# Operand loads of two output projections and row loads of a convolution's tail issued one step ahead, and one tail begun later, in a one-layer fp32 decoder kernel

## The chip, the cores and the metric

The kernel runs on 1 core of one Trainium2 chip. The metric is the device time of one execution in microseconds (us). Three runs of the kernel before gave 2037.54, 2042.94 and 2036.72 us; their median is 2037.54.

The engines have short names in the profile: PE is the matmul engine (PEld its weight loads), DVE the vector engine, ACT the scalar engine, POOL the GpSimd engine, SP the engine whose instruction stream issues most DMAs. A name with a q, such as SPq or ACTq, is the queue from which an engine issues DMAs. Each engine runs its own instructions in the order in which they stand; engines wait for each other on semaphores.

## The reference

One decoder layer over 2048 rows of 1024 values, all float32. Shortened:

```python
hn    = rms_norm(x, mix_pre_g)
proj  = hn @ w_in                               # q, k, v and the convolution's GLU input
attn  = sliding_window_attention(q, k, v, ...)  # window 128, 8 heads, 512 columns
conv  = silu(layer_norm(depthwise_conv31(a * sigmoid(gate)))) @ w_conv_pw   # 512 columns
mixed = concatenate([attn, conv]) @ w_out
h     = x + rms_norm(mixed, mix_post_g)
hn    = rms_norm(h, ffn_pre_g)
ff    = (silu(hn @ w_gate) * (hn @ w_up)) @ w_down
out   = h + rms_norm(ff, ffn_post_g)
```

## The kernel before

The 2048 rows are four tiles of T = 512 rows, numbered 0 to 3. A matmul of float32 accuracy is made of three: each operand is split into a rounded high part (ACT, `AF.Copy`) and a remainder (DVE or POOL, a subtraction), and high x high, high x low and low x high are added up in one PSUM bank.

The names of the stages are labels that the program gives to its tiles. A0 to A3 are the input projections. T0 to T3 are the convolution's taps: 30 multiply-adds per chunk of 128 channels on DVE, four chunks per tile; a finished chunk is stored to a DRAM array `y_scr` (L570). C0 to C3 are the convolution's tails. B is the attention. W0 to W3 are the output projections with their norms, N1 and N3 the later part of such a norm. F0 is the first half of the feed-forward for tiles 0 and 1, G0 the second half (`stage_p2`, L1103), F2 and G2 the same for tiles 2 and 3. H2 prepares operands of F2.

The change lies in what runs beside G0. G0 makes 7 products of 11 steps each, so 77 steps; in a step it loads one block from `mids` (L1122, tiles fa@G and at@G) and, every other step, two from `td` or `w_down` (L1126, mb@G), splits them (two ACT copies, two DVE subtractions, hl@G) two steps ahead, and multiplies with 12 matmuls, three into each of four banks. After the last step of a product, `after` (in `stage_p2`) empties the four banks by copies or additions on DVE and ACT (p@G, x@G) before the next product may write there. The product that ends with step 65 is emptied by additions into x@G on DVE.

Work of other stages runs between the steps in *lanes*. A lane holds a list of generators. Each step of the main stage gives every lane some time (`pump`, about L1275): the lane has a credit that grows by this time multiplied by its rate, and it resumes its first generator while the credit is positive. What a generator yields is taken off the credit. So `yield 0.5` is a price that decides how much main work passes before the next piece. A lane's item may have a condition: `since(lane, name, d)` holds when that item of that lane ended at least d of this planned time ago. These prices set the order in which instructions are emitted; a scheduler of the tile framework orders each engine's instructions with a model of its own. It decides the order in the queues on the chip.

While G0 runs, the lane `lw` holds in this order C2, W2, C3, W3, B11.2 (part of H2), and N3 is added by W3. The lane `lc` runs the last taps, T3.

**The tail, `stage_tail` (L573) and `conv_tail` (L588).** For each of four chunks it loads a row block from `y_scr` into a tile fc@C (L582, 256 KB on SP's queue), transposes it with four matmuls (`turn`, L550 to L557, PE line L554, ct@C) and copies the bank to yt@C (L555). Then `conv_tail` takes mean and variance on DVE (L594, L595), a reciprocal square root (`rsqrt`, L150, on POOL when `beside_taps`, lines L159 to L162), waits for its lane, transposes back (L607), applies the activation and multiplies by `w_pw` (four products `three`), whose results go to the DRAM array `mixT` through ACT's queue.

**The output projection, `stage_w` (L693).** It goes through the 8 chunks of mixT (four of the attention, four of the convolution) in groups of G = 2. For a group, `acts` loads two blocks at@W from `mixT` (L702, SP's queue, 256 KB each), copies the high part (L704, ACT, ql@W) and subtracts the low part (DVE). Each group has two column halves n = 0, 1 of `block_half` (L667): for each of four row groups, six matmuls into a bank tr@W, which is copied or added into mid@W (L675 and DVE). The weights raw@W and w@W are loaded by `weight` (L140).

**The norm, `norm_w` (L732).** It loads the gain gb@W (L684), sums squares (L738, ACT), takes `rsqrt` (on POOL for tiles 0 to 2, on DVE for tile 3), scales with eight DVE operations (`post_scale`, L688: mid@W<-mid@W,sm@W,gb@W), adds rows of x (L757, L759), stores h (h_scr), sums squares again (L760), and takes a second `rsqrt`. `stage_h_plain` (L814) reads such rows back transposed (tr@H, L800), and stores hT<-gb@H (L821) from tiles gb, of which there are two, shared with gb@W.

**The outputs of G0, `finish` (L1081):** norms the pairs of rows, loads h back (wx@G, L1095) and stores `out` (L1099).

The constants: CS = 10 is the planned time between the end of a tile's taps and the start of its tail (the condition on C3), Q0 = 8 the number of early units of F0 that run within W1.

Of the kernel before, what the change touches and what calls it, by code (L numbers as in the profile page):

```python
# [26 lines left out]
T = 512  # L27
NT = S // T
KC = D // P
# [8 lines left out]
def layer_kernel(ctx, tc, x, xT, cols, rows, sinks, relb, onehot, w_in, w_pw, w_out, w_gate, w_up, w_down, out):  # L38
    nc = tc.nc
# [7 lines left out]
    lab = ["X0"]  # L47
# [7 lines left out]
    def t_(tag, shape, dt=F32):  # L55
        return sb.tile(list(shape), dt, tag=tag, name=nm(tag), bufs=BUFS[tag])

    def f4(tag, shape=(P, D)):
        return t_(tag, shape)

    def f2(tag, shape=(P, T)):
        return t_(tag, shape)

    def hl(tag):
        return t_(tag, (P, 2, T), F32R)
# [74 lines left out]
    def weight(src, low, made, raw=None, on_pool=True):  # L140
        if raw is None:
            raw = t_("raw", (P, 2, T))
            nc.sync.dma_start(raw, src)
        return [split_w(raw[:, n], "w", low[n], made, on_pool) for n in range(2)]
# [85 lines left out]
    mixT = dr.tile([KC, P, S], F32, name="mixT")  # L230
# [17 lines left out]
    y_scr = dr.tile([4, P, S], F32, name="y_scr")  # L248
# [301 lines left out]
    def turner(yt, ycs):  # L550
        def turn(c):
            b = ct()
            for s in range(4):
                nc.tensor.transpose(b[:, s * P : (s + 1) * P], ycs[c][:, s * P : (s + 1) * P], ident)  # L554
            act(yt[:, :, c * P : (c + 1) * P], b.rearrange("p (s c) -> p s c", c=P), AF.Copy)  # L555

        return turn  # L557
# [15 lines left out]
    def stage_tail(t):  # L573
        L = f"C{t}"
        lab[0] = L
        yt = t_("yt", (P, 4, 4 * P))
        ycs = []
        turn = turner(yt, ycs)
        for c in range(4):
            lab[0] = L  # L580
            y = f2("fc")
            nc.sync.dma_start(y, y_scr[c, :, t * T : (t + 1) * T])  # L582
            ycs.append(y)
            turn(c)
            yield 0.5
        yield from conv_tail(t, yt)

    def conv_tail(t, yt):  # L588
        L = f"C{t}"
        lab[0] = L  # L590
        mv = sm(8).rearrange("p (s a) -> p s a", a=2)
        for s in range(4):
            st = sm(6)
            nc.vector.bn_stats(st, yt[:, s])  # L594
            nc.vector.bn_aggr(mv[:, s], st)  # L595
        r = rsqrt(mv[:, :, 1], 4, 1.0)
        nmr = sm(4)
        stt(nmr, mv[:, :, 0], -1.0, r, ALU.mult, ALU.mult)
        yield YL if t < 2 else YL2
        lab[0] = L  # L600
        for s in range(4):
            act(yt[:, s], yt[:, s], AF.Identity, scale=r[:, s : s + 1], bias=nmr[:, s : s + 1])
        sc = []
        for c in range(4):
            b = ct()
            for s in range(4):
                nc.tensor.transpose(b[:, s * P : (s + 1) * P], yt[:, s, c * P : (c + 1) * P], ident)  # L607
            th = f2("fc")
            act(th, b, AF.Tanh, scale=lnh[:, c : c + 1], bias=lnh[:, 4 + c : 5 + c])
            v = f2("fc")  # L610
            act(v, b, AF.Identity, scale=ln_g[:, c : c + 1], bias=ln_b[:, c : c + 1])
            stt(v, th, 1.0, v, ALU.add, ALU.mult)
            h = hl("chl")
            act(h[:, 0], v, AF.Copy)
            ptt(h[:, 1], v, h[:, 0].bitcast(F32), ALU.subtract)
            sc.append(h)
            yield 2
            lab[0] = L
        for m in range(4):
            raw = f2("fc")  # L620
            nc.sync.dma_start(raw, w_pw[m])
            w = split_w(raw, "mb" if t == 1 and m % 2 else "chl").rearrange("p a (k c) -> p a k c", c=P)
            o = ct()
            three(o, [((w[:, 0, k], w[:, 1, k]), (sc[k][:, 0], sc[k][:, 1])) for k in range(4)])
            z = f2("gb" if t > 1 else "fc")
            act(z, o, AF.Copy, scale=0.5)
            nc.scalar.dma_start(mixT[4 + m, :, t * T : (t + 1) * T], z)
            yield 2
            lab[0] = L
# [37 lines left out]
    def block_half(acc, units, n, first, L, bank_of, s0=0):  # L667
        cs = slice(n * T, (n + 1) * T)
        for i in range(len(acc)):
            s = i + s0  # L670
            lab[0] = L
            o = bank_of()
            three(o, [((a[s // 4][:, 0, ss(s)], a[s // 4][:, 1, ss(s)]), (w[:, 0], w[:, 1])) for a, w in units])
            if first:
                act(acc[i][:, cs], o, AF.Copy)  # L675
            else:
                vtt(acc[i][:, cs], acc[i][:, cs], o, ALU.add)
            yield 0.65 * len(units)
# [14 lines left out]
    def stage_w(w, spill, G, atag, htag, mtag, bank_of, norm=None, ready=None):  # L693
        L = f"W{w}"
        lab[0] = L
        acc = [f4(atag) for _ in range(4)]

        def acts(gi):
            aa = []
            for c in range(G * gi, G * gi + G):  # L700
                m = f2(mtag)
                nc.sync.dma_start(m, mixT[c, :, w * T : (w + 1) * T])  # L702
                a = hl(htag)
                act(a[:, 0], m, AF.Copy)  # L704
                vtt(a[:, 1], m, a[:, 0].bitcast(F32), ALU.subtract)
                aa.append([a])
            return aa

        nxt = acts(0)
        for gi in range(KC // G):  # L710
            aa = nxt
            for n in range(2):
                lab[0] = L
                if n == 1 and gi + 1 < KC // G and not (ready and G * gi + G == 4):
                    nxt = acts(gi + 1)
                ws = weight(w_out[2 * gi : 2 * gi + 2, :, n * T : (n + 1) * T].rearrange("c p t -> p c t"),
                            lo_out[n, 2 * gi : 2 * gi + 2], w > 0)
                yield from block_half(acc, list(zip(aa, ws)), n, gi == 0, L, bank_of)
            if ready and G * gi + G == 4:
                for i, c in enumerate(ready()):  # L720
                    if i == Q0 // 2:
                        ld.until("C1")
                        lab[0] = L
                        nxt = acts(gi + 1)
                    yield c
        tail = norm_w(w, spill, acc, mtag)
        if norm:
            norm(tail)
        else:
            yield from tail  # L730
# [526 lines left out]
    def since(lane, name, dt):  # L1257
        return name in lane.done and clk[0] >= lane.done[name] + dt
# [51 lines left out]
    TAPS0 = 6  # L1310
    NWARM = 9
    FILL = (2, 2, 2, 2, 2, 1, 0, 0)
    CS = 10
    YC = 3
    YP = 1.5
    YL, YL2 = 12, 20
# [5 lines left out]
    Q0 = 8  # L1322
# [5 lines left out]
    lc = Lane(RC0, LC)  # L1328
    lw = Lane(RW0, 0)
# [19 lines left out]

    lb.add("X", stage_x(), lambda: "x1" in started)  # L1350
    lw.add("W0", stage_w(0, True, 2, "x", "hl", "fa", mm), lambda: "A3" in started and "C0" in ld.done)
    TGA = [["hl"] * 8, ["mid"] * 4 + ["chl"] * 4, ["hl"] * 8, ["mid"] * 4 + ["hl"] * 4]
    xa = {}
# [6 lines left out]
    for t in range(2):  # L1360
        ld.add(f"C{t}", stage_tail(t), lambda t=t: since(lc, f"T{t}", CS))
    for t in range(NT):
# [39 lines left out]
    for n, off in (("B11", 0), ("B21", 4)):  # L1402
        lh.add(n + ".0", stage_h_plain(ws, ops, n, off))
    run(stage_w(1, True, 2, "mid", "hl", "at", mm, norm=lambda g: lh.add("N1", g), ready=lambda: stage_pre(ws, ops, mids[0], keeps[0], 0, Q0)))
    lc.hold = lambda: "S0" not in lh.done
    lh.until("B21.0")
# [6 lines left out]
    lc.rates["T3"] = RC3  # L1413
    ws, ops = (2, 3), {}
    lw.add("C2", stage_tail(2))
    lw.add("W2", stage_w(2, True, 2, "mid", "ql", "at", tr))
    lw.add("C3", stage_tail(3), lambda: since(lc, "T3", CS))
    lw.add("W3", stage_w(3, True, 2, "mid", "ql", "at", tr, norm=lambda g: lw.add("N3", g)))
    lw.add("B11.2", stage_h_plain(ws, ops, "B11", 0))
    run(stage_p2((0, 1), mids[0], td))  # L1420
# [70 lines left out]
```

## Time and profile before

| | us |
|---|---|
| median of 3 runs | 2037.54 |
| runs, lowest to highest | 2036.72 to 2042.94 |
| the profiled execution | 2046.33 |
| its span, first to last instruction | 2044.6 |
| granted TensorE clock, mean over the span | 0.984 |

Durations and times of the trace are those of the one profiled execution; a time such as 1202.57 counts in us from the start of the span. In a timeline row the columns are start, duration, engine, source line, operation, output<-inputs, shapes, and the number of instructions drawn together; in square brackets stand the idle time of the engine before them and what ended it. L85 and L108 are lines of helpers: every DVE operation through `dve` and every matmul of a three-part product have these lines, so the tile names tell them apart. The letter behind the @ is the stage without its number.

The profile has the kernel read 330.60 MB from HBM and write 119.02 MB, 220 GB/s over the span.

### The profile page before, as it was taken

How to read it: one execution, taken by the hardware profiler on the slowest of the kernel's cores; microseconds unless marked ns; L12 is line 12 of the kernel's file. 1: busy time of each engine (PE TensorE's matmuls, PEld its weight loads, DVE VectorE, ACT ScalarE, POOL GpSimd, SP SyncE). 2: the span in 40 equal slices, each digit the busy share in tenths (PEclk: the TensorE clock that was granted, in tenths of full speed). 3: DMA queues.
4: the chain of work that ended last, by engine and by line, in shares of the span. 5: the costliest groups of instructions: out<-in, count | busy, mean ns of one | idle time of the engine just before them, and what ended most of it. 6: DMA issues, size and time to landing. Idle time of an engine off the chain costs nothing. (4 is left out here: it accounts for less than half of the span.)

```text
span 2044.6 us, 27163 instructions
## 1 busy us (share of the span) xinstructions
PE 1961.9 (96%) x8826; PEld 1569.7 (77%) x8826; DVE 1501.3 (73%) x2641; ACT 986.3 (48%) x1938; POOL 399.3 (20%) x442
## 2 busy tenths in 40 slices
PE   8999999999989999999989999989999999999997
PEld 6877766776667778787878778877788888888886
DVE  5999896995885799888649985576756665545558
ACT  5355455456546633333346457555733433345543
POOL 4011223333111300000001012104523333221001
PEclk9999999999999999999999999999999999999999
DMA  8787645678559877777386788579954453366654
GB/s 307 255 300 232 203 135 184 184 240 277 186 156 326 272 239 241 257 247 244 130 263 209 229 266 279 191 278 302 348 169 161 149 169 114 103 235 214 206 186 149
DMA packets 235902, 451.44 MB, mean 221 GB/s; under 512 B 23496, under 2 KB 49264, under 8 KB 235760
## 3 DMA queue, kind: packets, MB, share of 16 engines
q1 hardware_dynamic: 215216, 419.30, 62.6%
q10 hardware_dynamic: 20544, 30.42, 4.0%
q8 instruction: 69, 1.13, 0.2%
q14 instruction: 73, 0.60, 0.1%
HBM read 330.60 MB, written 119.02 MB: 220 GB/s over the span
## 5 line engine op out<-in xcount | busy, mean ns | idle before, releaser
L85 DVE SCALAR_TENSOR_TENSOR fc@C<-glu@C,colt,fc@C 128x512 f32<-128x512 f32 x480 | 368.7, 781 | 3.5
L108 PE MATMUL mm@F<-hl@H,w@F 128*128 128x512 f32 x1056 | 255.2, 393 | 3.6 <-ACT mm@F L909 3.6
L108 PE MATMUL mm@G<-hl@G,hl@G 128*128 128x512 f32 x924 | 229.0, 397 | 9.8 <-DVE x@G L85 5.4
L108 PEld LDWEIGHTS mm@F<-hl@H,w@F 128*128 128x128 f32 x1056 | 200.4, 190 | 45.9 <-ACT mm@F L909 4.1
L108 PE MATMUL mm@A<-hl@A,w@A 128*128 128x512 f32 x840 | 206.9, 398 | 6.0 <-ACT w@A L133 1.7
L108 PEld LDWEIGHTS mm@G<-hl@G,hl@G 128*128 128x128 f32 x924 | 173.9, 191 | 48.6 <-ACT hl@G L782 7.9
L782 ACT ACTIVATE w@F<-chl@F 128x512 fp32r<-128x512 f32 x220 | 135.6, 625 | 148.9 <-PE mm@F L108 140.7
L108 PE MATMUL mm@G<-w@G,hl@G 128*128 128x512 f32 x876 | 199.6, 389 | 0.8 <-DVE w@G L85 0.8
L108 PEld LDWEIGHTS mm@G<-w@G,hl@G 128*128 128x128 f32 x876 | 164.4, 188 | 35.2 <-DVE w@G L85 1.2
L108 PEld LDWEIGHTS mm@A<-hl@A,w@A 128*128 128x128 f32 x840 | 155.9, 189 | 42.6 <-DVE hl@A L85 2.4
L85 DVE TENSOR_TENSOR w@F<-chl@F,w@F 128x512 fp32r<-128x512 f32 x198 | 144.9, 734 | 34.7 <-ACT w@F L782 34.3
L108 PE MATMUL mm@F<-mid@H,w@F 128*128 128x512 f32 x528 | 133.2, 396 | 3.3 <-ACT mm@F L909 3.3
L108 PE MATMUL mm@F<-ql@H,w@F 128*128 128x512 f32 x528 | 127.8, 390 | 5.8 <-ACT w@F L782 5.7
L108 PE MATMUL mm@F<-p@H,w@F 128*128 128x512 f32 x528 | 132.3, 397 | 0.0
L108 PE MATMUL mm@F<-x@H,w@F 128*128 128x512 f32 x528 | 127.4, 395 | 2.3 <-ACT fa@F L931 2.3
L108 PEld LDWEIGHTS mm@F<-ql@H,w@F 128*128 128x128 f32 x528 | 98.8, 188 | 27.3 <-ACT w@F L782 6.5
L108 PEld LDWEIGHTS mm@F<-mid@H,w@F 128*128 128x128 f32 x528 | 99.2, 189 | 26.4 <-ACT mm@F L909 5.4
L108 PEld LDWEIGHTS mm@F<-x@H,w@F 128*128 128x128 f32 x528 | 99.8, 190 | 24.0 <-ACT fa@F L931 2.8
L108 PEld LDWEIGHTS mm@F<-p@H,w@F 128*128 128x128 f32 x528 | 101.2, 192 | 22.1 <-ACT at@F L1031 0.8
L108 PE MATMUL mm@W<-w@W,hl@W 128*128 128x512 f32 x384 | 102.4, 412 | 7.6 <-ACT hl@W L704 7.3
L133 ACT ACTIVATE w@A<-raw@A 128x512 fp32r<-128x512 f32 x110 | 67.6, 626 | 84.4 <-PE mm@A L108 52.4
L108 PE MATMUL tr@W<-w@W,ql@W 128*128 128x512 f32 x384 | 98.5, 395 | 5.8 <-ACT mid@W L675 4.6
(299 smaller groups left out, 3376.9 us busy)
## 6 DMA issues: line engine op xcount, KB each, us to landing
mids<-fa@F SPq DMA_DIRECT2D x154, 256.0 KB, 2.7
raw@A<-w_in SPq DMA_DIRECT2D x55, 512.0 KB, 4.6
w@A<-lo_in SPq DMA_DIRECT2D x84, 256.0 KB, 3.5
fc@G<-mids SPq DMA_DIRECT2D x77, 256.0 KB, 3.4
fa@G<-mids SPq DMA_DIRECT2D x75, 256.0 KB, 4.5
gb@F<-keeps SPq DMA_DIRECT2D x72, 256.0 KB, 4.6
raw@W<-w_out SPq DMA_DIRECT2D x32, 512.0 KB, 5.6
w@W<-lo_out SPq DMA_DIRECT2D x48, 256.0 KB, 4.1
```

Of the source, the lines that this page charges most:

```text
L85: r = op(*args, **kw)
L108: r = nc.tensor.matmul(*args, **kw)
L133: act(w[:, 0], raw, AF.Copy)
L782: act(w[:, 0], x, AF.Copy)
```

## The change

Three edits.

1. `stage_tail`, for tiles 2 and 3 (`t > 1`): the load of the first chunk is issued alone, then the generator yields 2.0. In each turn the load of the next chunk is issued before the transposes of the present one. A turn yields 1.0 instead of 0.5.
2. `stage_w`: `acts` is cut into `loads` (the DMAs) and `acts` (the splits). For tiles 2 and 3 (`w > 1`) the generator yields 4.0 between the first loads and the first splits, and for each later group the loads are issued with the first column half (n = 0) of the group before, the splits with its second half (n = 1). For tiles 0 and 1 both stay at n = 1. In tile 1's special path (`ready`) the loads stay at unit Q0 // 2 = 4 and the splits move to unit Q0 - 2 = 6.
3. C3 may start 16 instead of 10 of planned time after T3 (`CS3`).

```diff
@@ stage_tail
+        def fetch(c):
+            if c < 4:
+                lab[0] = L
+                ycs.append(f2("fc"))
+                nc.sync.dma_start(ycs[c], y_scr[c, :, t * T : (t + 1) * T])
+
+        if t > 1:
+            fetch(0)
+            yield 2.0
         for c in range(4):
-            lab[0] = L
-            y = f2("fc")
-            nc.sync.dma_start(y, y_scr[c, :, t * T : (t + 1) * T])
-            ycs.append(y)
+            fetch(c + (t > 1))
+            lab[0] = L
             turn(c)
-            yield 0.5
+            yield 1.0 if t > 1 else 0.5
         yield from conv_tail(t, yt)
@@ stage_w
-        def acts(gi):
+        def loads(gi):
+            lab[0] = L
+            ms = []
+            for c in range(G * gi, G * gi + G):
+                ms.append(f2(mtag))
+                nc.sync.dma_start(ms[-1], mixT[c, :, w * T : (w + 1) * T])
+            return ms
+
+        def acts(ms):
+            lab[0] = L
             aa = []
-            for c in range(G * gi, G * gi + G):
-                m = f2(mtag)
-                nc.sync.dma_start(m, mixT[c, :, w * T : (w + 1) * T])
+            for m in ms:
                 a = hl(htag)
...
-        nxt = acts(0)
+        ms = loads(0)
+        if w > 1:
+            yield 4.0
+        nxt = acts(ms)
         for gi in range(KC // G):
             aa = nxt
+            own = gi + 1 < KC // G and not (ready and G * gi + G == 4)
             for n in range(2):
                 lab[0] = L
-                if n == 1 and gi + 1 < KC // G and not (ready and G * gi + G == 4):
-                    nxt = acts(gi + 1)
+                if n == (w < 2) and own:
+                    ms = loads(gi + 1)
+                if n == 1 and own:
+                    nxt = acts(ms)
...
                     if i == Q0 // 2:
                         ld.until("C1")
-                        lab[0] = L
-                        nxt = acts(gi + 1)
+                        ms = loads(gi + 1)
+                    if i == Q0 - 2:
+                        nxt = acts(ms)
                     yield c
...
-    CS = 10
+    CS, CS3 = 10, 16
...
-    lw.add("C3", stage_tail(3), lambda: since(lc, "T3", CS))
+    lw.add("C3", stage_tail(3), lambda: since(lc, "T3", CS3))
```

## The prediction

> **What bounds the kernel now.** I read the page's shares first, then the busy time in stretches of 20 us, then PE's waits over 1040 to 1500 us, and last the timelines around each wait.
>
> ```profile
> span 2044.6 us, 27163 instructions
> PE 1961.9 (96%) x8826; PEld 1569.7 (77%) x8826; DVE 1501.3 (73%) x2641; ACT 986.3 (48%) x1938; POOL 399.3 (20%) x442
> ```
>
> The matmul engine sets the time: it is idle for 2044.6 - 1961.9 = 82.7 us in the whole span. The edit moves work and removes none, so it can gain only what PE waits for where the edit reaches. The instruction orders of the two kernels are the same on all engines up to about step 12 of the first second-half product (stage_p2, a step being 12 matmuls mm@G), some 1090 us into the trace, and again behind the first part of the second F stage, about 1500 us. The stretches in which PE was not full are these (columns: stretch, length, PE, PEld, DVE, ACT, POOL busy with counts, granted clock, DMA share, GB/s):
>
> ```profile
> 1180.00:1200.00 20.00, 19.37 (x90) 15.69 (x88) 16.99 (x30) 13.13 (x24) 5.10 (x12) 1.00 0.71 222
> 1200.00:1220.00 20.00, 17.33 (x71) 14.07 (x72) 18.30 (x36) 9.62 (x18) 1.48 (x4) 0.91 0.77 247
> 1340.00:1360.00 20.00, 14.37 (x58) 11.00 (x57) 16.92 (x27) 7.93 (x15) 0.00 (x0) 0.86 0.71 242
> 1380.00:1400.00 20.00, 17.51 (x83) 14.01 (x82) 13.71 (x21) 14.73 (x30) 15.25 (x30) 1.00 0.76 247
> 1420.00:1440.00 20.00, 19.92 (x88) 16.14 (x87) 5.59 (x8) 10.52 (x19) 5.17 (x4) 1.00 1.03 374
> ```
>
> and PE's waits between 1040 and 1500 us, with one of ACT's (us in total, times, longest):
>
> ```profile
> PE mm@G L108 <- DVE x@G L85: 5.4, 1, 5.4
> PE tr@W L108 <- ACT mid@W L675: 4.6, 1, 4.6
> PE mm@F L108 <- ACT mm@F L909: 3.3, 5, 1.2
> PE ct@C L554 <- DMA fc@C<-y_scr: 3.2, 1, 3.2
> PE mm@G L108 <- DVE hl@G L85: 2.7, 3, 1.8
> PE tr@W L108 <- ACT ql@W L704: 1.2, 3, 0.7
> ...
> ACT ql@W L704 <- DMA at@W<-mixT: 44.0, 12, 6.5
> ```
>
> The edit's two loads stand in two very different rows. ACT waits 44.0 us for the output projection's operands, but PE waits only 1.2 us for ACT's result (ql@W): nearly all of that wait lies under the lanes' lead over PE. The row load of the convolution's tail costs PE 3.2 us, once. The 4.6 us lie at 1050 us, ahead of everything that the edit moves, and stay.
>
> **Wait 1, the row load at 1199 us.** Nothing is removed: the same four loads of 256 KB go out, the first without its transposes, each later one a turn ahead. In the new order the last transposes stand at step 36.0 (before 34.17). PE, then DVE, POOL and SP:
>
> ```profile
> 1195.81 3.56 PE L108 MATMUL mm@G<-hl@G,hl@G 128*128 128x512 f32 x15
> 1202.57 0.63 PE L554 MATMUL ct@C<-ident,fc@C 128*128 128x128 f32 x4 [3.20 <-DMA fc@C<-y_scr]
> 1203.29 25.47 PE L108 MATMUL mm@G<-hl@G,hl@G 128*128 128x512 f32 x104
> 1228.60 0.27 PE L607 MATMUL ct@C<-ident,yt@C 128*128 128x128 f32 x1
> 1329.46 19.32 PE L108 MATMUL mm@G<-hl@G,hl@G 128*128 128x512 f32 x84
> 1348.62 0.60 PE L800 MATMUL tr@H<-ident,fc@H 128*128 128x128 f32 x4
> ```
>
> ```profile
> 1194.17 0.74 DVE L85 SCALAR_TENSOR_TENSOR fc@C<-glu@C,colt,fc@C 128x512 f32<-128x512 f32 x1
> 1197.25 5.39 DVE L85 SCALAR_TENSOR_TENSOR mid@W<-mid@W,sm@W,gb@W 128x512 f32<-128x512 f32 x8 [2.33 <-POOL sm@W L162]
> 1207.30 0.68 DVE L85 TENSOR_TENSOR hl@G<-mb@G,hl@G 128x512 fp32r<-128x512 f32 x1
> 1191.21 0.57 POOL L159 TENSOR_TENSOR sm@W<-sm@W 128x4 f32<-128x4 f32 x1 [45.63 <-DVE sm@W L85]
> 1195.05 0.20 POOL L159 TENSOR_TENSOR sm@W<-sm@W 128x4 f32<-128x4 f32 x1
> 1197.02 0.20 POOL L162 TENSOR_TENSOR sm@W<-sm@W,sm@W 128x4 f32<-128x4 f32 x1
> 1194.94 0.32 SPq L570 DMA_DIRECT2D y_scr<-fc@C  x1
> 1199.27 0.32 SPq L582 DMA_DIRECT2D fc@C<-y_scr  x1
> ```
>
> An undisturbed matmul takes (1348.62 - 1329.46) / 84 = 0.228 us, a step 2.74. The 104 behind the wait took 1228.60 - 1203.29 = 25.31 instead of 23.7: 1.6 more, at a granted clock of 0.91. Wait 1 cost 4.8 in all. In the new order the store of the last row still goes out at about 1194.9, and the load 4.3 behind it as now, landing 3.3 later at 1202.6 (its transposes now start at 1202.57). The PE reaches them 22 matmuls later than now: 1199.37 + 22 x 0.228 = 1204.4. So the load is in time, by 1.8 us.
>
> What is late next is DVE. The norm of tile 2's projection moves from before step 33.5 to step 36.0, because its products end at step 31.67 instead of 29.1. Now its three POOL iterations (1191.21 to 1197.22, 6.0 us) lie beside the last taps; in the new order only one split (two subtractions, 1.2) stands between them and the eight scalings. DVE goes on every 0.6 (the four x@G additions below, 2.47): last tap done 1194.9, two copies 1.2, one split 1.2, three small operations 0.3: 1197.6. POOL's twelve: the eight from 1195.05 on, with DVE idle, came every 0.27, the first four every 0.96. Two beside the split at 0.96 and ten at 0.27 are 4.6, so 1202.3, or 1203.6 with the 6.0 as it was. Scalings 5.3, split of step 37 1.2: 1208.8 to 1210.1. PE would be there at 1199.37 + 0.72 (transposes) + 34 x 0.228 = 1207.8. A new stall of 1.0 to 2.3, and I take the upper, 2.3, since ACT's splits have to fit in too. With the clock's loss in proportion (1.6 x 2.3 / 3.2 = 1.2) wait 1 becomes 3.5 instead of 4.8: **-1.3**. Bounds: no stall at all, -4.8; a stall of 5.2 (taps ended 3 us later, since W2's additions are queued among them and PE makes their products later), with 1.6 of clock, +2.0.
>
> [...]
>
> Loads issued earlier wait at SP for their store, and the step loads fa@G and mb@G queue behind. That costs nothing while SP is some four steps (11 us) ahead of PE, and a store to landing takes about 3; without that cover each such wait would cost those 3. Behind step 37 DVE is at its edge now, and the additions of tile 2's rows and the convolution's norm move to 40 to 44.5: **+0.5**, between 0 and +2.
>
> **Wait 2, 1352 us: x@G behind tile 3's norm.** PE needs a bank at step 66, which DVE's x@G addition releases.
>
> ```profile
> 1337.86 0.33 SPq L684 DMA_DIRECT2D gb@W<-rows  x1
> 1340.79 0.33 SPq L684 DMA_DIRECT2D gb@W<-rows  x1
> 1342.30 2.74 DVE L85 SCALAR_TENSOR_TENSOR mid@W<-mid@W,sm@W,gb@W 128x512 f32<-128x512 f32 x4 [2.11 <-DMA gb@W<-rows]
> 1346.00 2.74 DVE L85 SCALAR_TENSOR_TENSOR mid@W<-mid@W,sm@W,gb@W 128x512 f32<-128x512 f32 x4 [0.96 <-DMA gb@W<-rows]
> 1356.42 2.47 DVE L85 TENSOR_TENSOR x@G<-x@G,mm@G 128x512 f32<-128x512 f32 x4
> 1349.40 2.40 PE L108 MATMUL mm@G<-hl@G,hl@G 128*128 128x512 f32 x8 [0.18 <-DVE hl@G L85]
> 1357.24 29.35 PE L108 MATMUL mm@G<-hl@G,hl@G 128*128 128x512 f32 x120 [5.44 <-DVE x@G L85]
> ```
>
> Starting C3 after 16 instead of 10 moves W3's last products from step 56.92 to 59.67 and the four groups of H transposes ahead of 1329.46 from 58.33 to 61.08: 2.75 steps, 7.5 us, nearer to step 66. From those transposes to the end of the scalings the chain took 1348.74 - 1329.46 = 19.3. Against that the first x@G addition no longer waits for five more splits and row additions (1348.74 to 1356.42 = 7.7): it comes right behind the second four scalings. Chain: 19.3 + 0.6 (first addition) + 0.4 (one row addition and a split, partly in the present waits for gb) = 20.3. PE: 59 matmuls (13.4) + four transposes (0.8) + 0.1 = 14.3. Stall 6.0 against 5.44: **+0.6**. The clock's loss, 29.19 - 120 x 0.228 = 1.8 by the start of the next row (1386.43), is the same. Bounds: -3.1 if the two gb waits (2.11 + 0.96) vanish; +5 if only a third of the 7.7 is really saved.
>
> **Wait 3, the end of that stage, 1387 to 1391 us.**
>
> ```profile
> 1386.43 0.27 PE L800 MATMUL tr@H<-ident,at@H 128*128 128x128 f32 x1
> 1389.03 0.96 PE L108 MATMUL mm@G<-hl@G,hl@G 128*128 128x512 f32 x3 [1.76 <-DVE hl@G L85]
> 1390.72 2.13 PE L108 MATMUL mm@G<-hl@G,hl@G 128*128 128x512 f32 x8 [0.73 <-DVE hl@G L85]
> ```
>
> The last splits are late behind the norm's end and the outputs' finish. In the new order all splits precede them: **-2.5**, between -2.7 and 0.
>
> **Behind it.** The outputs of this stage are finished later: before the second F stage's first kept block is loaded, SP has issued three stores and two wx loads, where it issued six and four. So 3 x 0.25 + 2 x 0.5 = 1.8 MB more lands in 1400 to 1480 us.
>
> ```profile
> out<-p@G SPq DMA_DIRECT2D x8, 256.0 KB, 4.2
> wx@G<-h_scr SPq DMA_DIRECT2D x7, 512.0 KB, 5.7
> ```
>
> There the DMA share is already 1.03 at 374 GB/s, so 1.8 MB are 4.9 us if all of it reaches PE; PE was busy 19.92 of 20 all the same, so a buffer of work covers transfers. I take **+1.5**, between 0 and +4.9.
>
> **Sum.** -1.3 + 0.5 + 0.6 - 2.5 + 1.5 = -1.2. The profiled execution, 2046.33 with its span of 2044.6, lay 8.8 above the median of 2037.54, so 2045.1 by its own measure and 2036.3 by the median's. The bounds add up to -10.6 and +13.9: 2027 to 2051.
>
> **The rivals.**
> Faster: neither new stall comes. The DVE window at 1180 to 1200 shows 3 us of idle time, enough to catch up; gb is already there when W3's chain is later. Then -4.8 - 3.1 - 2.5 + 1.5 = -8.9: 2028.6. Against it: POOL's 4.6 us have only 1.2 of DVE work beside them.
> Slower: tile 3's norm. All of its 7.5 us goes into PE at step 66, and the end of the stage is then pushed too, so wait 3 stays: -1.3 + 0.5 + 7.5 + 1.5 = +8.2, 2045.7. It decides from the point where the first x@G addition ends some 13 us (5.44 + 7.5) behind PE's last matmul of step 65; from 10.9 on the whole would be over 6 us slower (-1.3 + 0.5 + 1.5 + 5.4). For it: the gb loads were late already (1340.79 to 1346.00). Against it: the saved 7.7.
> Nothing happens to PE: the 44.0 us were all hidden, and the row load's 3.2 only become DVE's 3.2; 2037.5.
> The later outputs take the DMA: the sum with +4.9 in place of 1.5, 2039.7.
>
> **How the numbers follow.** A measurement of this kernel tells 0.3%, 6.1 us, from no change: 2031.4 to 2043.7. My forecast has 0.33, nothing happens 0.06, the DMA 0.05, faster 0.29, slower 0.27. The first three lie within it but for 0.01 of tail on either side: same 0.42, faster 0.30, slower 0.28. The range 2027 to 2049 leaves about 2 in 10 out; the forecast's own is 2031 to 2042.
>
> **What would show it.** In the new profile: PE's wait for fc@C<-y_scr gone; a wait of PE for hl@G of about 2 us near step 37, DVE waiting 3 to 4 us for POOL's sm@W in front of eight scalings; the x@G wait still 5 to 7 us; no wait for hl@G in the last two steps of the stage; ACT's 44.0 us for at@W<-mixT smaller without PE gaining as much. Wrong if DVE's splits stay ahead at step 37, if the x@G wait passes 10 or falls under 3, if waits for mm@F around 1460 us grow over 5 us, or if a wait appears between 1090 and 1190 us, where I count none.

## The result and the profile after

The changed kernel takes 2050.75 us (median of 6 runs, 2046.02 to 2056.37), the kernel before, in the same 6 rounds, 2038.43 us (2033.79 to 2042.94). The ratio on record is 1.0044, with a 95% interval of 1.0025 to 1.0063 (the two medians alone give 1.0060, inside it): the change costs 0.25 to 0.63%, 5 to 13 us. The forecast was no change, at 2036.3 us, with a range of 2027 to 2049.

The changed kernel's profiled execution ends 2.3 us after that of the kernel before (span 2046.9 against 2044.6). First the busy times, from its page:

```profile
span 2046.9 us, 27170 instructions
PE 1965.7 (96%) x8826; PEld 1572.0 (77%) x8826; DVE 1509.3 (74%) x2641; ACT 986.1 (48%) x1938; POOL 394.6 (19%) x442
```

Its busy time in the stretches that were shown of before, and in the one from 1220 to 1240 us:

```profile
1180.00:1200.00 20.00, 18.89 (x87) 15.33 (x86) 19.79 (x34) 11.86 (x22) 0.89 (x2) 1.00 0.69 232
1200.00:1220.00 20.00, 19.48 (x87) 15.40 (x85) 16.35 (x28) 8.55 (x15) 2.21 (x11) 1.00 0.67 211
1220.00:1240.00 20.00, 17.88 (x70) 13.49 (x70) 14.78 (x32) 13.58 (x25) 5.81 (x21) 0.91 0.99 338
...
1340.00:1360.00 20.00, 14.83 (x61) 12.01 (x61) 14.95 (x26) 7.47 (x14) 0.00 (x0) 0.87 0.74 243
...
1380.00:1400.00 20.00, 19.86 (x94) 16.26 (x93) 13.84 (x25) 15.15 (x31) 13.26 (x20) 1.00 0.50 179
...
1420.00:1440.00 20.00, 17.26 (x69) 14.11 (x70) 9.08 (x16) 8.93 (x17) 4.66 (x4) 0.91 0.97 349
```

In the kernel before, the added stretch was:

```profile
1220.00:1240.00 20.00, 20.00 (x94) 16.51 (x93) 11.95 (x24) 15.57 (x25) 7.69 (x21) 1.00 0.95 344
```

PE gained 2.15 us at 1200 to 1220 and 2.35 at 1380 to 1400, where two of its waits were expected to go. It lost 2.12 at 1220 to 1240 and 2.66 at 1420 to 1440, two stretches that were full before (20.00 and 19.92). PE's waits from 1040 to 1520 us in the changed kernel (us in total, times, longest):

```profile
PE mm@G L108 <- DVE x@G L85: 5.7, 2, 5.2
PE tr@W L108 <- ACT mid@W L682: 5.1, 1, 5.1
PE mm@F L108 <- DVE w@F L85: 4.0, 1, 4.0
PE mm@F L108 <- ACT mm@F L930: 3.0, 2, 2.6
PE ct@C L614 <- ACT yt@C L609: 1.4, 2, 1.1
...
PE mm@G L108 <- DVE p@G L1176: 1.1, 1, 1.1
...
PE mm@G L108 <- DVE hl@G L85: 0.5, 1, 0.5
```

The row load's wait (ct@C for fc@C<-y_scr, 3.2) is gone, and most of the wait for hl@G (2.7, now 0.5). New are waits of 1.4 us for yt@C and 1.1 for p@G, and a longer one: the products of the second F stage, F2, wait 4.0 us for a split of their weights on DVE. The timelines of the changed kernel show it: PE first, then DVE's queue in front of that split.

```profile
1422.74 17.79 PE L108 MATMUL mm@F<-ql@H,w@F 128*128 128x512 f32 x70 [3.95 <-DVE w@F L85]
```

```profile
1406.22 0.68 DVE L85 TENSOR_TENSOR w@F<-raw@F,w@F 128x512 fp32r<-128x512 f32 x1
1406.83 1.25 DVE L85 TENSOR_TENSOR sm@G<-sm@G 128x2 f32<-128x2 f32 x1
1408.11 2.63 DVE L85 TENSOR_SCALAR sm@G<-sm@G 128x2 f32<-128x2 f32 x3
1410.77 1.20 DVE L85 TENSOR_TENSOR sm@G<-sm@G 128x2 f32<-128x2 f32 x1
1412.01 2.46 DVE L85 SCALAR_TENSOR_TENSOR sm@G<-sm@G,sm@G 128x2 f32<-128x2 f32 x2
1414.50 0.16 DVE L85 TENSOR_TENSOR sm@G<-sm@G 128x2 f32<-128x2 f32 x1
...
1420.61 0.74 DVE L85 SCALAR_TENSOR_TENSOR p@G<-p@G,sm@G,wx@G 128x512 f32<-128x512 f32 x1
1421.27 0.74 DVE L85 SCALAR_TENSOR_TENSOR x@G<-x@G,sm@G,wx@G 128x512 f32<-128x512 f32 x1
1421.93 0.15 DVE L85 TENSOR_TENSOR sm@G<-sm@G 128x2 f32<-128x2 f32 x1
1422.00 0.68 DVE L85 TENSOR_TENSOR w@F<-raw@F,w@F 128x512 fp32r<-128x512 f32 x1
```

Between two splits that F2 needs lie 15.1 us of the *finish* of stage G0's outputs (`finish`, tiles sm@G, p@G, x@G): two chains of square roots and their scalings, with a few other operations of the stage's end. In the kernel before, the same queue reached its splits in time:

```profile
1413.15 0.68 DVE L85 TENSOR_TENSOR w@F<-raw@F,w@F 128x512 fp32r<-128x512 f32 x1
...
1417.73 0.69 DVE L85 TENSOR_TENSOR w@F<-raw@F,w@F 128x512 fp32r<-128x512 f32 x1
...
1423.26 0.69 DVE L85 TENSOR_TENSOR w@F<-raw@F,w@F 128x512 fp32r<-128x512 f32 x1 [3.44 <-ACT w@F L782]
```

The wait costs more than its length: the 70 matmuls behind it took 17.79 us, 1.8 more than 70 x 0.228, at a granted clock of 0.91 in the stretch of 1420 to 1440 us. Together 5.8 us.

**Where in the run.** The two spans hide this. The two kernels' orders are the same up to G0, and yet the start of the last unit of the first F stage (the 1801st matmul mm@F) lay at 1026.6 us in the profile of before and at 1022.8 in that of the change; over all profiles of this study that point moved from 1020.3 to 1031.1 us. So the stages are compared from that point on. The table, worked out from the start times in the traces, gives how much later than in the first profile of the kernel before each kernel reaches the last matmul of G0 and the 2501st of mm@F (in F2, at 1551.5 us in the kernel before); behind it, the ratio of times to the kernel before in the same rounds.

| kernel | end of G0 | in F2 | ratio (95% interval) |
|---|---|---|---|
| before, second profile | +0.5 | -0.5 | 0.9995 (0.9972 to 1.0019) |
| the change | +0.3 | +6.7 | 1.0044 (1.0025 to 1.0063) |
| cs3_alone (edit 3) | +0.3 | +10.5 | 1.0040 (1.0022 to 1.0057) |
| tail_alone (edit 1) | +2.1 | +9.6 | 1.0043 (1.0028 to 1.0057) |
| w_alone (edit 2) | -0.2 | +4.8 | 1.0027 (1.0011 to 1.0044) |
| after_cs10 (edits 1, 2) | -3.2 | +4.7 | 1.0016 (1.0004 to 1.0028) |
| after_hold4 | -1.1 | +10.0 | 1.0028 (1.0014 to 1.0042) |
| after_rspool | -1.2 | +6.9 | 1.0013 (1.0000 to 1.0026) |
| cs10_actcopy | -2.0 | +5.9 | 1.0029 (1.0016 to 1.0043) |
| after_rw135 | -0.4 | +7.1 | 1.0007 (0.9993 to 1.0022) |
| after_pooldma | -1.0 | +7.7 | 1.0044 (1.0032 to 1.0056) |
| before_bare | +0.6 | -5.3 | 0.9961 (0.9946 to 0.9977) |
| after_bare | -2.4 | -8.2 | 0.9955 (0.9940 to 0.9971) |
| after_dmaonly | 0.0 | -4.2 | 0.9966 (0.9953 to 0.9979) |
| after_nowx | -0.6 | +9.5 | 1.0015 (0.9999 to 1.0030) |
| after_late | -4.6 | +11.4 | 1.0110 (1.0088 to 1.0131) |
| before_late | -0.8 | +11.8 | 1.0092 (1.0077 to 1.0107) |
| after_late2 | -0.9 | +2.3 | 1.0051 (1.0038 to 1.0065) |
| before_late2 | -2.9 | 0.0 | 1.0065 (1.0043 to 1.0087) |

From G0's start to its end the change costs nothing in sum (0.3, where the second profile of the kernel before gives 0.5). It loses 6.4 us from there into F2. The columns come from one execution each, the ratios from many: the profile of after_rw135 lies 7.1 us late and its median does not, so single profiles tell where time goes, and the ratios how much. The ratios are of fast runs alone; two of after_nowx's 12 runs, of 3250 and 9142 us (the others 2041 to 2052), are left out, and nothing here explains them.

### The profile page after: what moved, and what is told of

It is laid out like the page before. It is cut to its first block, busy times and chain, and to the rows that moved or that the text cites. A ratio compares the mean times of both kernels' runs of the same rounds, so it can differ in the third digit from the quotient of the medians.

```text
span 2046.9 us, 27170 instructions
## 1 busy us (share of the span) xinstructions
PE 1965.7 (96%) x8826; PEld 1572.0 (77%) x8826; DVE 1509.3 (74%) x2641; ACT 986.1 (48%) x1938; POOL 394.6 (19%) x442
```

## The experiments

**Which edit?** Each edit was made alone, and the third taken out. Edit 3 alone is `CS, CS3 = 10, 16` with its condition; edit 1 alone is the new `stage_tail` in the kernel before, edit 2 alone the new `stage_w`. The last is:

```diff
-    CS, CS3 = 10, 16
+    CS, CS3 = 10, 10
```

> The kernel before with the third edit alone (C3 may start 16 instead of 10 after T3). In its instruction order W3's last products stand at step 59.2 of the first stage_p2 (before 56.9, after the change 59.7). Theory A (what costs is that the tail of tile 3 ends some 2.5 steps later, whichever edit moves it; the outputs' finish then runs into the start of the second F stage): ratio 1.003 to 1.006 (+6 to +12 us), a PE wait mm@F for DVE w@F of 3 to 5 us near 1420 us, the row-load wait of 3.2 gone or smaller. Rival B (the cost comes from tile 2's tail and projection, which edits 1 and 2 spread): ratio within 0.998 to 1.002. Rival C (the cost is C3's later start): ratio 1.004.

> The kernel before with the first edit alone (row loads of the tails of tiles 2 and 3 one step ahead, with their longer yields). W3's last products stand at step 59.3, tile 2's pointwise products at 21.4 to 27.3 (before 17.8 to 23.3). Theory A: ratio 1.003 to 1.006 with the wait for w@F. Rival B: 1.003 to 1.006 too. Rival C: 0.998 to 1.002.

> The kernel before with the second edit alone (loads of the output projection's operands ahead of their splits). W3's last products at step 59.2, tile 2's pointwise products at 18.1 to 23.5, nearly as before. Theory A: ratio 1.003 to 1.006 with the wait for w@F. Rival B: under 1.002, since tile 2 hardly moves. Rival C: 0.998 to 1.002.

> The changed kernel with C3's start put back to 10 (edits 1 and 2 together). W3's last products at step 59.3. Theory A: ratio 1.003 to 1.006. Rival B: 1.003 to 1.006. Rival C: 0.998 to 1.002.

Measured: 1.0040, 1.0043, 1.0027 and 1.0016. Rival B falls by cs3_alone (said: at most 1.002) and rival C by tail_alone (said: at most 1.002). The three single losses add up to 0.0110, and together they cost 0.0044, so this isn't a sum of prices. In all four W3's last products stand at step 59.2 to 59.3 (before 56.9). Theory A holds in part: each of the four profiles loses between G0's end and F2 (5.0 to 10.2 us by the table), and three of them lose nothing in G0 (tail_alone 2.1). But w_alone and after_cs10 cost less than the 1.003 that it gave, and it was too narrow about the place. PE waits at F2's first products in each (cs3_alone, w_alone, after_cs10; then tail_alone), not for w@F but for a bank:

```profile
1394.27 45.99 PE L108 MATMUL mm@F<-ql@H,w@F 128*128 128x512 f32 x189 [4.80 <-DVE p@G L1155]
```

```profile
1398.49 41.77 PE L108 MATMUL mm@F<-ql@H,w@F 128*128 128x512 f32 x183 [3.49 <-DVE p@G L1169]
```

```profile
1399.36 40.99 PE L108 MATMUL mm@F<-ql@H,w@F 128*128 128x512 f32 x169 [4.75 <-DVE p@G L1176]
```

```profile
1393.11 41.63 PE L108 MATMUL mm@F<-ql@H,w@F 128*128 128x512 f32 x180 [2.46 <-ACT p@G L1160]
```

DVE's queue of cs3_alone shows why:

```profile
1388.53 1.74 DVE L85 SCALAR_TENSOR_TENSOR p@G<-p@G,sm@G,wx@G 128x512 f32<-128x512 f32 x1 [3.34 <-POOL sm@G L162]
1390.19 1.75 DVE L85 SCALAR_TENSOR_TENSOR x@G<-x@G,sm@G,wx@G 128x512 f32<-128x512 f32 x1
1391.87 1.75 DVE L85 TENSOR_TENSOR mid@H<-gb@H,mid@H 128x512 fp32r<-128x512 f32 x1
1393.54 1.27 DVE L1155 COPY p@G<-mm@G 128x512 f32<-128x512 f32 x2
```

The copies that empty the banks of G0's last product stand behind two scalings of the finish, and these wait for POOL's square root. So the same work, the finish, hits F2 in one place or in another.

**Can the order alone be mended?** Four kernels moved one piece each. after_hold4 holds the finish's lane back, after_rspool puts a square root on POOL, cs10_actcopy (on after_cs10) puts the last copies on ACT, after_rw135 paces tiles 2 and 3 faster:

```diff
 # after_hold4
+    lf.hold = lambda: "P2.4" not in started
     run(stage_p2((0, 1), mids[0], td))
 # after_rspool
-        r = rsqrt(ssq[:, 0:n_], n_, 1, pool and L == "G0")
+        r = rsqrt(ssq[:, 0:n_], n_, 1, L == "G0")
 # cs10_actcopy
-                copy(b, home("c12", "p", b), o)
+                act(home("c12", "p", b), o, AF.Copy)
 # after_rw135
-    RC0, RC1, RC2, RC3, RW0, RW, RB, LC = 0.7, 1.1, 0.4, 0.9, 1.7, 1.25, 0.8, 100
+    RC0, RC1, RC2, RC3, RW0, RW, RB, LC = 0.7, 1.1, 0.4, 0.9, 1.7, 1.35, 0.8, 100
```

> The changed kernel with one lane held: the finish of stage G0's outputs may be emitted only from the fifth unit of the second F stage on. Its instruction order is that of the changed kernel up to DVE's third weight split w@F of the second F stage, which now stands ahead of the last six small operations and the two scalings of the outputs' norm, not behind them. Theory A (in the changed kernel PE's first F2 products wait for a w@F split that is queued on DVE behind the outputs' finish): the wait mm@F for DVE w@F falls from 4.0 to under 1.5 us, and the ratio to the kernel before from 1.0044 to 1.001 to 1.0025. Rival D (the time is lost elsewhere, for instance to DMA traffic of the later stores): the wait moves to another releaser and the ratio stays at 1.0035 or more.

> The changed kernel with the square roots of the even rows' outputs (18 small DVE operations, up to 1.2 us each in the profile) computed on POOL, as those of the odd rows are. Theory A: DVE reaches the third w@F split some 10 us sooner, the wait for it is gone, ratio 1.000 to 1.0025. Rival D: 1.0035 or more.

> Edits 1 and 2 without the third (measured 1.0016), and the four copies that empty the banks of G0's last product all on ACT instead of two on DVE. There PE waited 4.75 us for the first bank of F2, because DVE's two copies stood behind two scalings and these behind POOL's square root. Theory A: this wait falls to under 1.5 us and the time by 3 to 5 us, ratio 0.9985 to 1.0005. Rival D: the next wait (w@F) takes its place and the ratio stays at 1.0010 or more.

> The changed kernel with the lane of tiles 2 and 3 paced faster (rate 1.35 instead of 1.25): W3's last products come at step 58.0 instead of 59.7, the scalings of its norm at 65 to 66 instead of 67 to 68, and the outputs' finish starts before the last splits, nearly as in the kernel before. Theory A in its wide form (what counts is how late tile 3's projection ends): ratio 0.999 to 1.002. Narrow form (only DVE's order at the first F2 products counts): the x@G wait gets 1 to 3 us shorter, a wait at F2's first products remains, ratio 1.001 to 1.003. Rival D: 1.004.

Measured: 1.0028, 1.0013, 1.0029, 1.0007. Each wait that was aimed at became shorter, but in the first three one of 1.9 to 2.5 us still stood at nearly the same time: in after_hold4 the same wait for w@F (said: under 1.5), in the others one for another operation. PE at 1420 to 1423 us in after_hold4, in after_rspool and in cs10_actcopy:

```profile
1420.12 17.80 PE L108 MATMUL mm@F<-ql@H,w@F 128*128 128x512 f32 x70 [2.32 <-DVE w@F L85]
```

```profile
1423.08 15.07 PE L108 MATMUL mm@F<-ql@H,w@F 128*128 128x512 f32 x58 [1.91 <-POOL w@F L807]
```

```profile
1422.00 18.25 PE L108 MATMUL mm@F<-ql@H,w@F 128*128 128x512 f32 x72 [2.49 <-ACT fa@F L952]
```

cs10_actcopy missed its forecast: removing the 4.75 us in front bought nothing (1.0029 against 1.0016 without it, intervals overlapping). Its last wait leads to ACT, which stood still for 7.5 us in front of a copy that needs nothing of the finish:

```profile
1413.19 0.62 ACT L803 ACTIVATE w@F<-raw@F 128x512 fp32r<-128x512 f32 x1
1420.98 0.33 ACTq L953 DMA_DIRECT2D keeps<-fa@F  x1
1421.35 0.60 ACT L952 ACTIVATE fa@F<-mm@F 128x512 f32<-128x512 f32 x1 [7.54 <-DMA wx@G<-h_scr]
```

The profile puts these 7.54 us down to a load of the finish, wx@G, which SP issued at 1416.76. DVE's scaling that reads the load waits for it too and starts at 1420.93, and ACT's store `keeps` is issued at 1420.98. In the changed kernel's trace SP's 1359 DMAs and ACT's 100 signal the same eight semaphores, and one store of `keeps` is issued there at 1421.44, 0.07 us after a load of glu@G on SP with the same semaphore has landed, with 2.56 us of idle time on ACT put down to that load. That the store in cs10_actcopy waited for wx@G in the same way is the author's reading of its rows. And the load stood on SP behind a store of `out`, issued at 1416.10, 0.03 us after DVE's scaling had ended (1414.22 + 1.85). after_hold4 (1.0028) can't be told from the change (1.0044). after_rspool (1.0013) and after_rw135 (1.0007) are faster than it. after_rw135 has W3's end at step 58.0 and the finish begun before G0's last splits, and it can't be told from the kernel before; it still waits 3.3 us for a bank at F2's first products.

**Is it the finish?** It was left out for tiles 0 and 1, in both kernels: the products' rows are stored as they come.

```diff
         lab[0] = L
+        if L == "G0":
+            for rows_, halves in jobs:
+                lab[0] = L
+                for n in range(2):
+                    nc.sync.dma_start(out[rows_, n * T : (n + 1) * T], halves[n])
+                yield 4.0
+            return
         n_ = len(jobs)
```

> The kernel before without the finish of the outputs of tiles 0 and 1: their rows are stored as the product leaves them, so the norm over the feed-forward's output, its gain and the addition of h are left out for these tiles (squares on ACT, products on POOL and DVE, square roots, loads of h; the stores stay). Its instruction order within G0 is that of the kernel before. It gives what the finish costs there. Theory A: 0.996 to 0.999, since the waits of F2's first part and those of G0's last steps go (2 to 7 us).

> The changed kernel with the same finish left out (norm, gain and addition of h for the outputs of tiles 0 and 1). Theory A (the 9 us are lost because the finish stands in front of F2's first work, on DVE, on SP's queue and through the DMA semaphores that ACT's stores share with SP's loads): the ratio to the kernel before equals that of the kernel before without its finish within 0.0015, that is, the change's loss is gone. Rival E (the change loses its time inside G0 itself, or by other traffic): the loss of 0.0044 stays between the two bare kernels (0.003 or more).

Measured: 0.9961 and 0.9955. This settles that the loss needs the finish. Without it the change's loss of 0.0044 is gone; the changed kernel is then, if anything, the faster one (by 0.0006, inside both intervals). The finish costs the kernel before 0.4% and the changed one 0.9%, so what the change costs is the difference: the same finish in a worse place.

**Its arithmetic, its traffic or its queue?** after_dmaonly keeps the finish's DMAs and leaves its arithmetic out, after_nowx keeps the arithmetic and leaves out the loads of h (the row itself is added), after_pooldma issues its DMAs from POOL's queue.

```diff
 # after_dmaonly, in finish for G0
+                ht = f4("wx")
+                nc.sync.dma_start(ht, h_scr[rows_])
+                for n in range(2):
+                    nc.sync.dma_start(out[rows_, n * T : (n + 1) * T], halves[n])
 # after_nowx
-            nc.sync.dma_start(ht, h_scr[rows_])
+            if L != "G0":
+                nc.sync.dma_start(ht, h_scr[rows_])
 # after_pooldma (the stores of out likewise)
+        q = nc.gpsimd if L == "G0" else nc.sync
-            nc.sync.dma_start(ht, h_scr[rows_])
+            q.dma_start(ht, h_scr[rows_])
```

> The changed kernel whose outputs of tiles 0 and 1 keep the finish's DMAs (load of h, four stores of 256 KB per pair of rows) but none of its arithmetic: squares, gain, square root, scaling and addition of h are left out. Arithmetic theory (the finish's operations on DVE, POOL and ACT, in the order of their queues, delay F2's first splits and copies): as without the whole finish, 0.994 to 0.9975. Traffic theory (its loads and stores collide with F2's first weights): 1.001 to 1.0045.

> The changed kernel with the finish's arithmetic and stores, but without the loads of h (for tiles 0 and 1 the scaled row itself is added in place of h). Arithmetic theory: 1.001 to 1.0045, with a PE wait for a DVE result (w@F, p@G) of 2 us or more in F2's first 40 us. Traffic theory, its load part: 0.996 to 0.999.

> The changed kernel with the finish's own DMAs (stores of out, loads wx of h) issued from POOL's queue instead of SP's for tiles 0 and 1. Theory A, its queue path (SP's later loads and, over the shared semaphores, ACT's stores wait behind a store that waits for DVE): ACT's waits for wx@G<-h_scr in F2 vanish, ratio 1.000 to 1.0025. Its DVE path alone: the wait for DVE w@F of 4 us stays, ratio 1.0035 or more.

Measured: 0.9966, 1.0015, 1.0044. The stretch from 1400 to 1440 us in after_dmaonly, in after_nowx, in the changed kernel and in the kernel before:

```profile
1400.00:1440.00 40.00, 40.00 (x181) 33.06 (x179) 7.62 (x11) 22.12 (x39) 10.30 (x8) 1.00 1.00 349
```

```profile
1400.00:1440.00 40.00, 37.28 (x163) 30.23 (x163) 27.49 (x52) 21.06 (x46) 18.36 (x22) 1.00 0.91 300
```

```profile
1400.00:1440.00 40.00, 36.05 (x152) 29.31 (x152) 27.37 (x51) 22.84 (x49) 19.32 (x23) 0.96 0.97 342
```

```profile
1400.00:1440.00 40.00, 39.92 (x176) 32.72 (x175) 23.10 (x48) 21.30 (x42) 12.94 (x10) 1.00 1.00 345
```

With all the traffic and none of the arithmetic, PE is full at a DMA share of 1.00. With the arithmetic and less traffic it isn't. The changed kernel moves no more bytes here than the kernel before (342 and 345 GB/s); it has 4.3 us more of DVE and 6.4 more of POOL in this stretch. So in the changed kernel the arithmetic carries most of the finish's cost: from bare to DMAs only 0.0011, from bare to arithmetic and stores 0.0060, to the whole finish 0.0089. The rest of 0.0018 would be what the two cost only together, but four ratios enter it, each uncertain by 0.0013 to 0.0019, so it can't be told from nothing. after_pooldma, where the loads and the stores are on POOL's queue, is as slow as the change and kept a wait of 3.0 us for w@F.

One limit: the finish of the kernel before, which costs 0.0039, was not divided in this way. So it is shown that the finish carries the change's 0.0044, and not how these 0.0044 divide between its arithmetic and its loads; without the loads of h the changed kernel stands at 1.0015 (0.9999 to 1.0030), a third of the change's loss.

**Put the finish elsewhere.** In the later part of F2 PE is full and DVE is busy for some 60% of the time (469 and 280 of 470 us from 1560 to 2030 in the kernel before). In after_late and before_late the rows go unscaled to a scratch array and are normed there; in after_late2 and before_late2 the loads are also tied to the products beside them, so that the scheduler can't pull them forward.

```diff
+    lf.add("LATE", finish_late(), lambda: "S2" in lh.done)
     run(stage_p1(ws, ops, mids[1], keeps[1]))
+    lf.until("LATE")
 # late2, in finish_late
+                tied(nc.sync.dma_start(hs[n], fin[rows_, n * T : (n + 1) * T]))
```

> The changed kernel with the finish of the outputs of tiles 0 and 1 moved: the rows are stored unscaled to a scratch array as they come, and loaded, normed, added to h and stored again during the later, longer part of F2. Arithmetic theory: F2's start runs as without the finish, and the moved work lies under PE: 0.995 to 0.999, faster than both kernels. If the added 8 MB of traffic or DVE's work bind there: 1.000 or more.

> The kernel before with the same move of the finish. Theory A: within 0.0015 of the changed kernel with the move (the change itself then costs nothing); 0.996 to 0.999.

> The changed kernel with the finish of tiles 0 and 1 moved again, but its loads tied to the products of F2's later, long part (one pair of half rows about every 40 us), so that the scheduler can't pull them forward into F2's first part, where the last two kernels lost 16 us between 1440 and 1565 us. Theory A: 0.995 to 0.999, faster than both kernels. If the moved work binds in the later part: over 1.000, with PE waits behind 1565 us.

> The kernel before with the same tied move. Theory A: within 0.0015 of the changed kernel with it; 0.995 to 0.999.

Measured: 1.0110, 1.0092, 1.0051, 1.0065. As a better kernel the move failed, all four times. What it was asked about the change holds: with the finish moved the two kernels are equal within their intervals (0.0018 and -0.0014 apart, each with some 0.0026 either way). Where it lost shows in after_late2 from 1580 to 1660 us, where the kernel before has PE at 80.00 of 80:

```profile
1580.00:1660.00 80.00, 73.60 (x308) 59.35 (x308) 61.35 (x91) 30.78 (x59) 31.07 (x21) 0.96 0.58 194
```

```profile
PE mm@F L108 <- DVE fa@F L85: 5.1, 3, 3.3
PE mm@F L108 <- DVE gb@F L85: 2.2, 1, 2.2
```

The second fence lists PE's waits behind 1560 us: banks that DVE empties. DVE is busy for three quarters of that stretch. It seems that a few more operations in front of a bank's addition in its queue stop PE; no run here takes them out one by one.

**The yardstick.** 

> The kernel before once more, for a second profile: how far PE's time from the end of the first F stage to the second half of F2 repeats from run to run. All theories: ratio 1.000 within 0.002; that stretch within 2 us of the first profile.

Measured: 0.9995, and both points of the table within 0.5 us. Single stretches repeat less well, by up to 2.1 us (next section). No version tried here beats the kernel before with the whole output computed.

## Why the prediction was wrong

The forecast put the time inside 2027 to 2049 and expected no change; the median came to 2050.75 and the ratio's interval begins above 1. The step that failed is the last term of the sum, "Behind it": +1.5 us, at most 4.9, for transfers. Measured in the one pair of profiles it is +6.0, and what costs it is the finish that comes with the transfers. A second term, +0.5 behind step 37, was +4.3.

The table redoes the sum from the start times. It counts the time that PE lost: the time between two points less 0.227 us for each matmul of 512 columns (the median from one start to the next in the kernel before) and 0.108 for each transpose of 128 columns (there, 0.43 us from the start of four at 1328.67 to the next four at 1329.10). The columns give how much more than in the first profile of the kernel before.

| stretch | said | the change | before, second profile |
|---|---|---|---|
| steps 0 to 12, where both orders are the same | | +2.8 | +1.3 |
| steps 12 to 32 | none | +0.5 | -1.1 |
| steps 32 to 38, wait 1 | -1.3 | -3.0 | +0.2 |
| steps 38 to 65, behind step 37 | +0.5 | +4.3 | 0.0 |
| steps 65 to 75, wait 2 | +0.6 | -0.7 | -1.4 |
| step 75 to F2's first product, wait 3 | -2.5 | -3.1 | +2.1 |
| F2's first product to the 2501st of mm@F, behind it | +1.5 | +6.0 | -1.6 |

From step 12 to F2's first product the sum came out at -2.1 where -2.7 was said. That is luck: three terms gained 3.6 us more than said, and the two others lost 4.3 more. The second profile shows that a stretch repeats within about 2 us, so only +4.3 and +6.0 stand well clear of that, and -3.0 and -3.1 by a little. From step 12 on the pair of profiles differs by 3.9 us and the ratio says 5 to 13; the profiles show where, not the whole of it. The rows of the changed kernel, PE's and one of DVE's:

```profile
1210.86 12.26 PE L108 MATMUL mm@G<-hl@G,hl@G 128*128 128x512 f32 x52 [0.52 <-DVE hl@G L85]
...
1230.06 0.33 PE L614 MATMUL ct@C<-ident,yt@C 128*128 128x128 f32 x1 [1.06 <-ACT yt@C L609]
...
1231.63 2.76 PE L108 MATMUL mm@G<-hl@G,hl@G 128*128 128x512 f32 x6 [0.54 <-DVE x@G L85]
...
1356.94 32.38 PE L108 MATMUL mm@G<-hl@G,hl@G 128*128 128x512 f32 x132 [5.17 <-DVE x@G L85]
```

```profile
1203.07 5.39 DVE L85 SCALAR_TENSOR_TENSOR mid@W<-mid@W,sm@W,gb@W 128x512 f32<-128x512 f32 x8 [2.88 <-POOL sm@W L162]
```

Point by point:

- **Wait 1, the row load.** Right in mechanism. The load is in time, DVE waits 2.88 us for POOL's sm@W in front of the eight scalings (said: 3 to 4), the scalings start at 1203.07 (worked out: 1202.3), and a new stall comes at step 37, 0.52 us for hl@G (said: 2.3). The stall was oversized: PE lost 1.0 us between the starts of steps 37 and 38, where the prediction had 3.5. A wait of 1.1 us for a copy of p@G, at 1196.72, wasn't foreseen. The granted clock is 1.00 from 1200 to 1220 us, so the loss of clock in proportion was not there. In the kernel before, 1.6 us were lost behind the wait of 3.20, at a clock of 0.91 in the same stretch. The length of the longest wait doesn't tell in these rows whether the clock falls: behind the one of 1.11 it stayed at 1.00, and behind those of the next point, none over 1.06, it was 0.50.
- **Behind step 37.** Undersized, +0.5 with a bound of 2. ACT writes tile 2's normed rows, yt@C, from 1229.19 on (before: 1223.86), and PE comes to its transposes back at 1229.0 (before: 1228.6), so that norm, which had been some 5 us ahead of PE, now holds it up. From 1223 to 1232 us PE has four waits (0.15 to 1.06, 2.1 in all), and behind them the granted clock is 0.50 from 1232 to 1235 us, though no wait is longer than 1.06. Only two transposes ran on PE between 1229.0 and 1231.6.
- **Wait 2, x@G.** Right: 5.17 us at step 66 (said 6.0, before 5.44). The first x@G addition did come right behind the second four scalings. The slower rival, which put all of tile 3's delay here, fell.
- **Wait 3, the end of G0.** Right: the two waits for hl@G are gone, -3.1 (said -2.5, at most -2.7).
- **Behind it.** This step failed. The prediction saw that the outputs of G0 are finished later, counted the transfers that this moves into F2's start (1.8 MB, +1.5 us, at most 4.9), and put the arithmetic that moves with them at nothing. after_dmaonly shows the transfers at a DMA share of 1.00 with PE full; the two bare kernels show that without the finish the loss is gone. In the changed kernel's profile it is 3.95 us of wait for a weight split behind the finish on DVE, and 1.8 of slower matmuls. The prediction named what is queued for wait 1 and wait 2, but not what is queued behind the finish on DVE: F2's weight splits and the copies that free its banks. So the sum's bound of +4.9 for this term was no bound.
- **The chances** gave slower 0.28, for a mechanism that didn't come. A wait for mm@F near F2's start was named as what would make the prediction wrong, but around 1460 us; it came at 1422, and the two waits for mm@F's own copies stayed at 3.0 us. ACT's wait for at@W stayed too, 43.6 us (said: smaller than 44.0).

Left open: how the change's 0.0044 divides between the finish's arithmetic and its loads (with ACT's wait for a DMA of SP, 2.56 us in the changed kernel, and SP's queue); and why after_late2's DVE order could not be spread without stalls.

## What to carry to other kernels

Follow moved work to the end of the chain that it starts: here a tail, tile 3's, that came 2.75 steps later cost nothing where it ran, and moved the stage's last, uncritical norm onto the next stage's first splits and bank copies, on engines' queues with no slack at that moment (PE waited 3.95 us). Where mending one wait brings up another of about the same length at the same time, take the suspected work out altogether and see whether the loss goes; that settled here what four mended orders could not. And compare profiles stretch by stretch, from a point behind the part that is the same, with a second profile of the same kernel beside them: these spans differed by 2.3 us, the last stretch by 6.0, and one kernel's two profiles by up to 2.1 in a stretch.

## What was not expected of the hardware

DVE operations on 128x2 values took 0.15 to 0.17 us each, and 1.15 to 1.25 us when they began while POOL ran one of its 128x512 products: in the rows of the changed kernel above, the same form takes 1.25 us at 1406.83, 1.20 at 1410.77 and 0.16 at 1414.50, and POOL's products cover the first two:

```profile
1406.32 1.73 POOL L1109 TENSOR_TENSOR p@G<-p@G,glu@G 128x512 f32<-128x512 f32 x1
...
1410.67 1.29 POOL L807 TENSOR_TENSOR w@F<-raw@F,w@F 128x512 fp32r<-128x512 f32 x1
1411.91 2.54 POOL L1109 TENSOR_TENSOR p@G<-p@G,glu@G 128x512 f32<-128x512 f32 x2
```

A slow one ends when POOL's product ends: 1406.83 + 1.25 against 1406.32 + 1.73, and 1410.77 + 1.20 against 1410.67 + 1.29, within 0.03 us each, as if the small operation waited for the large one to finish. Between the two splits of 15.1 us there are eight such operations in the changed kernel, 9.7 us together; at 0.16 each they would be 1.3. The difference of 8.4 us, an estimate from these rows, is more than PE's wait of 3.95 for the second split. No run here takes POOL's products away; after_rspool, which takes the small operations off DVE instead, had a wait of 1.9 in that place.

In the stretch of 1395 to 1423 us twelve operations of one form (sm@G<-sm@G,sm@G) took 1.9 us in the kernel before and 5.1 in the changed one. Of the one-input form (TENSOR_SCALAR, 2.63 us for three at 1408.11) two are as slow, 1.17 and 1.22 us. What makes them slow, no row shows. Beside POOL's products a square root chain on tiny operands was not small here.
